# A Mamba-2 state-space branch, computed with channels instead of time steps on the partitions

## The chip, the core and the metric

The kernel runs on one core of a Trainium2 chip. A core has five engines that run at the same time, each working off its own instructions in order: TensorE multiplies matrices (in the profile PE, its weight loads PEld), VectorE (DVE) and ScalarE (ACT) do elementwise work, GpSimd (POOL) does elementwise work on the on-chip memory SBUF only, and SyncE (SP) issues DMAs. ACT can issue DMAs too. A matrix product writes into the accumulators, PSUM, and reads both operands from SBUF. SBUF and PSUM have 128 partitions; a tile `128x512` has 512 elements on each of them. In a product the *stationary* operand is loaded into the array first and the *moving* operand then streams through it. The metric is the time of one execution in microseconds (us).

## What is computed

One residual layer over 256 tokens of 2048 channels. A normalised input `h` is projected by one large matrix; the columns go to three branches (stick-breaking attention, a state-space branch, attention into 256 memory tokens), each branch is projected back to 2048 channels, the three are merged with sigmoid gates, and a last projection, a residual add and a norm follow. The change concerns the state-space branch. It has 32 heads of 64 channels in 8 groups of 4 heads (so a group is 256 channels), and one chunk of all 256 tokens:

```python
xbc = silu(causal_depthwise_conv(ssd_xbc, conv_w, conv_b))       # x, B, C
dt  = softplus(ssd_dt + dt_bias);  a = -exp(a_log)
xs  = x * dt[..., None];           a_cum = cumsum(dt * a)        # over time
decay_in = exp(where(tri, a_cum[l] - a_cum[s], -inf))
cb     = einsum('lgn,sgn->gls', C, B)
y      = einsum('gls,gels,sgep->lgep', cb, decay_in, xs)
y      = y + d_skip * x
g      = y * silu(z)
g      = g * rsqrt(mean over the group's 256 channels of g*g + eps) * ssd_norm_w
branch = g @ w_branch_ssd
```

The weights are f32. A large product is made exact by splitting both operands into a high and a low part (`wh`, `wl`; type f32r) and adding three products.

## The kernel before

**Chunks and pumps.** All weights stream from DRAM. A *chunk* is 512 KB of weights: SP loads it into one of four `raw` buffers (`load_chunk`, L205), ACT writes its high part `wh` (L144), DVE the low part `wl` (L148: `raw` minus `wh`), each into one of three buffers, and PE multiplies. `gemm` (L247) takes chunks of 2 x 128 input channels by 512 outputs and puts tokens on the partitions of the result; the activations are stationary, the weights move: twelve matmuls of 512 columns (L264 to L266). `gemm_cols` (L209) takes 4 x 128 input channels by 256 outputs and puts output channels on the partitions; the weights are stationary: eight matmuls of 512 columns (L227) and eight of 256 (L231). After each chunk's matmuls the program calls `pump` (L183), so a *pump* is the place between two chunks where other work is put into the engines' queues.

**Lanes.** Side work is written as generators. `pump` first runs what was deferred to this pump (`defer`), then advances one of two lanes, odd and even pumps in turn, by one step, up to the next `yield`. Where a generator ends, the next in its lane starts in the same advance. `finish` (L191) runs both lanes to their end at once.

**State space before.** `z` comes from four `gemm` of 8 chunks, evacuated by rows into `zD` (L675); `x`, `B`, `C` come from `gemm_cols`, go through the convolution and SiLU and stand by channels in `cT`. `dt_steps` (L447) leaves `dts` (dt), `nac` (minus the cumulated decay), `edge` (two exponentials of it) by time, and the cumulated decays by heads in DRAM, `acT`. `start_ssd`, eight pumps after the convolution's last chunk, fills each lane with four groups (`ssd_group`, L713), then four `ssd_cols` (L790).

A group takes nine advances: (1) transpose `x` into `xp` and load decays of all 256 tokens, spread over the partitions, through ACT's DMA queue; (2) copy `xp` (ACT), form `xs`, the skip term and `xoff` on POOL, multiply B and C into `cb`; (3) eight additions with minimum on DVE (L751); (4) Exp on ACT; (5) multiply by `cb`, masked, on DVE; (6) the products `y`, decays stationary, 64 columns of `xs` moving (L769), for each head two diagonal blocks of 128 x 128 tokens; what the first half of the tokens gives the second goes through `off` for the four heads together (L771); (7) add up and multiply by `z`, DVE; (8) squares with their sum on ACT, then on POOL mean plus epsilon (L137) and the power -0.5 (L138), `128x2`; (9) scale into `zD` (L786). `ssd_cols` transposes the finished rows back to channels on PE (`dot`, L799) and splits them with the norm's weight into `oD`, the operand of the branch's product. It starts when all eight groups are done.

**Around it.** During this the main program runs the loop over branches (L849): for each of four column blocks a gate `gemm` over `hT` (8 chunks) and a branch `gemm` (4, 4 and 8 chunks for memory, attention and state space). Ahead of the third branch stands `finish()` (L851), since that branch reads `oD`.

Of the kernel before, what the change touches and what calls it, by code (L numbers as in the profile page):

```python
# [10 lines left out]
F32 = mybir.dt.float32  # L11
F32R = mybir.dt.float32r
# [29 lines left out]
def trunk_kernel(  # L42
# [3 lines left out]
    d_skip, w_mem_kv, w_branch_sb, w_branch_ssd, w_branch_mem,  # L46
# [46 lines left out]
    wcols = const.tile([P, 192], F32, name="wcols")  # L93
    normw, ssdw, convb = wcols[:, 0:16], wcols[:, 16:32], wcols[:, 32:64]
    convw = wcols[:, 64:192].rearrange("p (j i) -> p j i", i=32)

# [27 lines left out]
    drow = const.tile([P, SSD_HEADS], F32, name="drow")  # L124

# [6 lines left out]
    edge = const.tile([P, 2, SSD_HEADS], F32, name="edge")  # L132
# [222 lines left out]
    def along(k):  # L355
# [14 lines left out]
        if k == 6:  # L370
            nc.sync.dma_start(wcols, w_cols)
            nc.sync.dma_start(drow, d_skip.partition_broadcast(P))
# [74 lines left out]
    def dt_steps():  # L447
# [54 lines left out]
        nc.vector.tensor_tensor(edge[:, 0], nac[:, 0], ps[:, 2], ALU.subtract)  # L502
        nc.vector.tensor_scalar(edge[:, 1], nac[:, 1], -1.0, None, ALU.mult)
        nc.scalar.activation(edge, edge, AF.Exp)
# [165 lines left out]
    zD = [slot([P, D], F32, "zD") for _ in range(2)]  # L670

    def z_evac(c0):
        def evac(acc):
            for t in range(2):
                nc.scalar.activation(zD[t][:, c0:c0 + GW], acc[t], AF.Copy)  # L675
        return evac

    for g in range(4):
        gemm(hT, NKT, w_in, C_SSDZ + g * GW, z_evac(g * GW))
# [20 lines left out]
    waiting = [zD[i // 2][:, (i % 2) * 1024:(i % 2 + 1) * 1024] for i in range(4)]  # L700
# [12 lines left out]
    def ssd_group(g):  # L713
        heads = slice(4 * g, 4 * g + 4)
        cs = slice(g * T, (g + 1) * T)
        xp = bank([P, 2, T], "xp")
        for b in range(2):
            i = 2 * g + b
            for t in range(2):
                nc.tensor.transpose(xp[:, t, b * P:(b + 1) * P],  # L720
                                    cT[i // 8][:, i % 8, t * P:(t + 1) * P], ident)
        dec = []
        for h0 in (4 * g, 4 * g + 2):
            d = ta([P, 2, 2, P], "dec")
            nc.scalar.dma_start(d.rearrange("p h q t -> p h (q t)"),
                                acT[h0:h0 + 2].partition_broadcast(P))
            dec.append(d)
        yield
        xn = tb([P, 2, T], "xn")
        nc.scalar.activation(xn, xp, AF.Copy)  # L730
        xs = tb([P, 2, T], "xs")
        xe = tq([P, 3, P], "xe")
        by_head = lambda a: a.rearrange("p (h c) -> p h c", c=64)
        wide = lambda a: a[:, heads].unsqueeze(2).to_broadcast([P, 4, 64])
        xoff = xe[:, 0:2].rearrange("p a b -> p (a b)")
        for t in range(2):
            nc.gpsimd.tensor_tensor(by_head(xs[:, t]), by_head(xn[:, t]), wide(dts[:, t]),
                                    ALU.mult)
            nc.gpsimd.tensor_tensor(by_head(xn[:, t]), by_head(xn[:, t]), wide(drow), ALU.mult)
        nc.gpsimd.tensor_tensor(by_head(xoff), by_head(xs[:, 0]), wide(edge[:, 0]), ALU.mult)  # L740
        cb = bank([P, 4, P], "cb")
        bT, cTT = cT[2], cT[3]
        nc.tensor.matmul(cb[:, 0:2], bT[:, g, 0:P], cTT[:, g], start=True, stop=True)
        nc.tensor.matmul(cb[:, 2], bT[:, g, P:T], cTT[:, g, P:T], start=True, stop=True)
        yield

        for i, d in enumerate(dec):
            for e in range(2):
                for q in range(2):
                    h = 4 * g + 2 * i + e  # L750
                    nc.vector.tensor_scalar(d[:, e, q], d[:, e, q], nac[:, q, h:h + 1], 0.0,  # L751
                                            ALU.add, ALU.min)
        yield
        for d in dec:
            nc.scalar.activation(d, d, AF.Exp)
        yield
        nc.scalar.activation(xe[:, 2], cb[:, 1], AF.Copy)
        cbm = small2([P, 2, P], "cbm")
        nc.vector.tensor_tensor(cbm, cb[:, 0:3:2], past.unsqueeze(1).to_broadcast([P, 2, P]),
                                ALU.mult)  # L760
        for d in dec:
            nc.vector.tensor_tensor(d, d, cbm.unsqueeze(1).to_broadcast([P, 2, 2, P]),
                                    ALU.mult)
        yield
        y = bank([P, 2, T], "y")
        for e in range(4):
            xc = slice(e * 64, (e + 1) * 64)
            for q in range(2):
                nc.tensor.matmul(y[:, q, xc], dec[e // 2][:, e % 2, q], xs[:, q, xc], start=True, stop=True)  # L769
        off = bank([P, T], "off")  # L770
        nc.tensor.matmul(off, xe[:, 2], xoff, start=True, stop=True)  # L771
        yield
        nc.vector.tensor_tensor(by_head(xoff), by_head(off), wide(edge[:, 1]), ALU.mult)
        nc.vector.tensor_tensor(xn[:, 1], xn[:, 1], xoff, ALU.add)
        nc.vector.tensor_tensor(xn, y, xn, ALU.add)
        ss = small([P, 2], "gss")
        for t in range(2):
            nc.vector.tensor_tensor(xn[:, t], xn[:, t], zD[t][:, cs], ALU.mult)
        yield
        for t in range(2):  # L780
            nc.scalar.activation(xs[:, t], xn[:, t], AF.Square, accum_out=ss[:, t:t + 1])
        rs = small([P, 2], "grs")
        rsqrt_mean(rs, ss, T, 2)
        yield
        for t in range(2):
            nc.scalar.activation(zD[t][:, cs], xn[:, t], AF.Copy, scale=rs[:, t:t + 1])  # L786
        ssd_done.append(g)
        yield

    def ssd_cols(g):  # L790
# [4 lines left out]
        ot = bank([P, 2, T], "dot")  # L795
        for b in range(2):
            c = (2 * g + b) * P
            for t in range(2):
                nc.tensor.transpose(ot[:, b, t * P:(t + 1) * P], zD[t][:, c:c + P], ident)  # L799
        yield  # L800
        split(*[(*oD[0].at(2 * g + b), ot[:, b], ssdw[:, 2 * g + b:2 * g + b + 1])
                for b in range(2)])
# [141 lines left out]
_INS = ['x', 'mem', 'x_cols', 'mem_cols', 'w_cols', 'w_in', 'b_gate', 'dt_bias', 'a_log', 'd_skip',  # L944
# [5 lines left out]
def lay_out(inputs):  # L950
# [8 lines left out]
    for name in ('x', 'mem'):  # L959
        a[name + '_cols'] = a[name].T.reshape(NKT, P, T).transpose(1, 0, 2).reshape(P, -1)  # L960
    a['mem_cols'] = _np.concatenate([a['mem_norm_w'].reshape(-1, P).T, a['mem_cols']], axis=1)
    a['w_cols'] = _np.concatenate([a[n].reshape(-1, P).T for n in
                                   ('norm_w', 'ssd_norm_w', 'conv_b', 'conv_w')], axis=1)
# [18 lines left out]
```

## Time and profile before

| | |
|---|---|
| median of 3 runs | 1232.03 us (1231.22 to 1232.85) |
| the profiled execution | 1232.29 us |
| its span, first to last instruction | 1230.6 us |
| granted TensorE clock, mean | 0.998 |
| busy: DVE, ACT, POOL | 769.0, 617.2, 92.2 us |
| DMA moved | 240.58 MB, mean 196 GB/s |

The page of the profile gives busy times and the chain of work that ended last; the chain is followed back from the last instruction, at each step to what released it. A group of instructions is written `line engine op out<-in`. In the timeline each row has start, duration, engine, line, operation, tiles, shape and count, and in brackets the idle time before it with what ended it. Matmuls are pipelined: a row's duration is longer than the distance to the next start, and it is the distance that adds up. A product of two f32 operands appears as two records in a trace, a transpose as one. A row of a line's own view has the shortest, median and longest duration in ns, then first and last start.

### The profile page before, as it was taken

What the parts mean: (1) busy time and instruction counts of PE and PEld (TensorE: products, weight loads), DVE (VectorE), ACT (ScalarE), POOL (GpSimd) and SP (SyncE); (2) the same over time, 40 slices, a digit from 0 to 9 for tenths busy, and PEclk for the clock granted to TensorE, in tenths of its full rate; (3) what the DMA queues carried; (4) which work ended last, traced back from release to release, by engine and by line L of the source; (5) the groups of instructions that cost most, each with busy time, mean ns of one, the idle gap of its engine ahead of it and who ended that gap; (6) DMA issues with size and microseconds to landing.
All of it is one profiled execution on the core that took longest, in us unless ns stands there. A gap on an engine that the chain in (4) does not pass through costs nothing.

```text
span 1230.6 us, 16254 instructions
## 1 busy us (share of the span) xinstructions
PE 1220.5 (99%) x6228; PEld 1037.9 (84%) x6228; DVE 769.0 (62%) x999; ACT 617.2 (50%) x797; POOL 92.2 (7%) x104
## 2 busy tenths in 40 slices
PE   9999999999999999999999999999999999999997
PEld 7888888888888888888888888888888888888886
DVE  5686554565654555888878767576756554555554
ACT  6765544554444554545664655455555444444443
POOL 0000000000000000010000202123101110110101
PEclk9999999999999999999999999999999999999999
DMA  9966566655566665655666756666565666567673
GB/s 339 334 198 188 163 195 189 187 168 166 165 183 191 178 177 179 184 176 171 178 182 201 226 178 207 204 191 198 180 186 180 198 197 200 187 197 243 205 243 109
DMA packets 165789, 240.58 MB, mean 196 GB/s; under 512 B 10288, under 2 KB 93392, under 8 KB 165584
## 3 DMA queue, kind: packets, MB, share of 16 engines
q1 hardware_dynamic: 157152, 223.88, 58.9%
q10 hardware_dynamic: 8560, 15.67, 3.8%
q8 instruction: 48, 0.79, 0.3%
q14 instruction: 29, 0.24, 0.1%
HBM read 237.40 MB, written 2.13 MB: 195 GB/s over the span
## 4 chain that ended last, share of the span: by engine, by line
PE 95%; DMA 2%; issue 1%; ACT 1%; DVE 1%; SPq 0%; POOLq 0%; POOL 0%; ACTq 0%
PE acc L227 24%; PE acc L264 17%; PE acc L266 17%; PE acc L265 17%; PE acc L231 12%; PE y L769 1%; PE acc L400 1%; PE acc L401 1%; PE acc L399 1%; DMA raw<-in_w_out_dram 1%; DMA rows<-in_mem_dram 1%; DMA raw<-in_w_mem_kv_dram 0%; PE off L771 0%; PE dtp L459 0%; PE dot L799 0%
## 5 line engine op out<-in xcount | busy, mean ns | idle before, releaser
L148 DVE TENSOR_TENSOR wl<-raw,wh 128x1024 fp32r<-128x1024 f32 (+1 forms) x409 | 506.0, 1240 | 326.4 <-ACT wh L144 324.1
L144 ACT ACTIVATE wh<-raw 128x1024 fp32r<-128x1024 f32 (+1 forms) x409 | 431.5, 1056 | 423.7 <-PE acc L266 253.7
L227 PE MATMUL acc<-hT,wh 128*128 128x512 f32 x1152 | 363.2, 397 | 0.0
L231 PEld LDWEIGHTS acc<-hT,wl 128*128 128x128 f32 x1152 | 216.4, 188 | 51.2
L264 PE MATMUL acc<-wh,hT 128*128 128x512 f32 x576 | 227.8, 395 | 0.0
L231 PE MATMUL acc<-hT,wl 128*128 128x256 f32 x1152 | 226.5, 278 | 0.0
L266 PE MATMUL acc<-wh,hT 128*128 128x512 f32 x576 | 224.5, 390 | 0.0
L265 PE MATMUL acc<-wl,hT 128*128 128x512 f32 x576 | 224.4, 390 | 0.0
L227 PEld LDWEIGHTS acc<-hT,wh 128*128 128x128 f32 x1152 | 175.5, 189 | 0.1
L266 PEld LDWEIGHTS acc<-wh,hT 128*128 128x128 f32 x576 | 108.1, 188 | 22.9
L265 PEld LDWEIGHTS acc<-wl,hT 128*128 128x128 f32 x576 | 108.3, 188 | 21.8
L264 PEld LDWEIGHTS acc<-wh,hT 128*128 128x128 f32 x576 | 108.2, 188 | 21.7
L265 PE MATMUL acc<-wl,oD 128*128 128x512 f32 x128 | 49.8, 389 | 0.0
L266 PE MATMUL acc<-wh,oD 128*128 128x512 f32 x128 | 49.8, 389 | 0.0
L264 PE MATMUL acc<-wh,oD 128*128 128x512 f32 x128 | 49.8, 389 | 0.0
L695 DVE SCALAR_TENSOR_TENSOR cT<-cu,wcols,cT 128x255 f32<-128x255 f32 (+2 forms) x96 | 46.4, 483 | 3.4
L841 POOL TENSOR_TENSOR merged<-merged,sig 128x512 f32<-128x512 f32 x16 | 27.5, 1743 | 260.7 <-DVE sig L840 233.9
L631 POOL TENSOR_TENSOR lm<-lm,sp 128x384 f32<-128x384 f32 x8 | 11.5, 1432 | 394.5 <-DVE sp L630 392.4
L227 PE MATMUL acc<-memT,wh 128*128 128x512 f32 x128 | 40.6, 398 | 0.0
L264 PE MATMUL acc<-wh,mT 128*128 128x512 f32 x96 | 37.4, 390 | 0.0
L266 PE MATMUL acc<-wh,mT 128*128 128x512 f32 x96 | 37.4, 389 | 0.0
L265 PE MATMUL acc<-wl,mT 128*128 128x512 f32 x96 | 37.4, 389 | 0.0
(250 smaller groups left out, 1306.1 us busy)
## 6 DMA issues: line engine op xcount, KB each, us to landing
raw<-in_w_in_dram SPq DMA_DIRECT2D x288, 512.0 KB, 3.8
raw<-in_w_branch_ssd_dram SPq DMA_DIRECT2D x32, 512.0 KB, 4.0
raw<-in_w_out_dram SPq DMA_DIRECT2D x32, 512.0 KB, 4.9
raw<-in_w_mem_kv_dram SPq DMA_DIRECT2D x31, 512.0 KB, 6.3
raw<-in_w_branch_mem_dram SPq DMA_DIRECT2D x16, 512.0 KB, 4.8
raw<-in_w_branch_sb_dram SPq DMA_DIRECT2D x16, 512.0 KB, 4.3
dec<-acT ACTq DMA_DIRECT2D x16, 256.0 KB, 5.6
sig<-in_b_gate_dram ACTq DMA_DIRECT2D x12, 256.0 KB, 3.9
```

Source lines behind the costliest of these rows:

```text
L144: nc.scalar.activation(hi, src, AF.Copy, **({} if scale is None else {"scale": scale}))
L148: nc.vector.tensor_tensor(lo, src, h32, ALU.subtract)
L227: nc.tensor.matmul(halves[b], wh[:, kt - k0, b * P:(b + 1) * P], lhs.both(kt), start=first, stop=False, skip_group_check=True)
L231: nc.tensor.matmul(halves[b][:, 1], wl[:, kt - k0, b * P:(b + 1) * P], lhs.at(kt)[0], start=False, stop=last, skip_group_check=True)
L264: nc.tensor.matmul(a, lh[:, tt], wh[:, j], start=first, stop=False)
L265: nc.tensor.matmul(a, lh[:, tt], wl[:, j], start=False, stop=False)
L266: nc.tensor.matmul(a, ll[:, tt], wh[:, j], start=False, stop=last)
L399: nc.tensor.matmul(a, lh[:, tt], wh[:, g], start=first, stop=False)
L400: nc.tensor.matmul(a, lh[:, tt], wl[:, g], start=False, stop=False)
L401: nc.tensor.matmul(a, ll[:, tt], wh[:, g], start=False, stop=last)
L695: nc.vector.scalar_tensor_tensor(a[:, s:T], u[:, 0:T - s], convw[:, 3 - s, i:i + 1], a[:, s:T], ALU.mult, ALU.add)
L841: nc.gpsimd.tensor_tensor(merged[t][:, cs], merged[t][:, cs], sig[:, t], ALU.add)
```

## The change

`z` is now computed by `gemm_cols` into `zT`, channels on the partitions, with the fold of two accumulators that `to_cols` does (a copy on ACT, an add on DVE). For each head three decay tiles of 128 x 128 are made, the third (first half of the tokens to second) in place of `off`; `edge` goes and `nacx` (`nac` of the first half less its end) comes. In the products `y` the 64 channels of a head in `xs` are stationary and the decays move; the even head of a pair writes partitions 0 to 63 of the result and the odd one 64 to 127. The result stands by channels, so that the skip term is one instruction per 128 channels with a per-partition scalar `dcol` (a column of `wcols`; the load of `drow` goes). The sum of squares over a group's channels is a product with a matrix of ones (`rb`, split operands `sq`), which gives `128x256` with all rows equal; DVE forms mean plus epsilon, POOL the power -0.5 over all 256 columns, DVE multiplies. POOL's five products a group go. `ssd_cols` only splits. A group takes eleven advances and each `ssd_cols` one. The decays are loaded by five DMAs a group from SP's queue instead of two from ACT's. `finish()` moves behind the third branch's first gate `gemm`.

```diff
-    for g in range(4):
-        gemm(hT, NKT, w_in, C_SSDZ + g * GW, z_evac(g * GW))
+    zT = [slot([P, 8, T], F32, "zT") for _ in range(2)]
+    for g in range(8):
+        gemm_cols(hT, NKT, w_in, C_SSDZ + 2 * g * P, to_cols(zT[g // 4], 2 * (g % 4)))
...
     def ssd_group(g):
...
+        dec = [ta([P, 4, P], "dec"), ta([P, 4, P], "dec"), tb([P, 4, P], "dec")]
+        block = lambda e, j: dec[e][:, j] if e < 3 else dec[j][:, 3]
+        for e in range(3):
+            nc.sync.dma_start(dec[e][:, 0:2].rearrange("p q t -> p (q t)"),
+                              acT[heads[e]:heads[e] + 1].partition_broadcast(P))
+        for j in range(2):
+            nc.sync.dma_start(dec[j][:, 3:4], acT[heads[3]:heads[3] + 1,
+                                                  j * P:(j + 1) * P].partition_broadcast(P))
...
+        nc.vector.tensor_tensor(by_head(xs), by_head(xp), dts[:, :, heads[0]:heads[0] + 4]
+                                .unsqueeze(3).to_broadcast([P, 2, 4, 64]), ALU.mult)
+        cbm = small2([P, 3, P], "cbm")
+        nc.scalar.activation(cbm[:, 1], cb[:, 1], AF.Copy)
+        nc.vector.tensor_tensor(cbm[:, 0:3:2], cb[:, 0:3:2],
+                                past.unsqueeze(1).to_broadcast([P, 2, P]), ALU.mult)
+        def log_decays(e):
+            for j, i, a in ((2, 1, nac[:, 1]), (1, 1, nacx), (0, 0, nac[:, 0])):
+                nc.vector.tensor_scalar(block(e, j), block(e, i), a[:, heads[e]:heads[e] + 1],
+                                        0.0, ALU.add, ALU.min)
+        def weigh(i):
+            nc.vector.tensor_tensor(dec[i][:, 0:3], dec[i][:, 0:3], cbm, ALU.mult)
+            nc.vector.tensor_tensor(dec[i][:, 3], dec[i][:, 3], cbm[:, i], ALU.mult)
+        log_decays(0)
+        yield
+        for e in (3, 1, 2):
+            log_decays(e)
+        nc.scalar.activation(dec[0], dec[0], AF.Exp)
+        yield
+        nc.scalar.activation(dec[1], dec[1], AF.Exp)
+        nc.scalar.activation(dec[2], dec[2], AF.Exp)
+        weigh(0)
+        yield
+        weigh(1)
+        weigh(2)
         yield
         y = bank([P, 2, T], "y")
-        for e in range(4):
-            xc = slice(e * 64, (e + 1) * 64)
-            for q in range(2):
-                nc.tensor.matmul(y[:, q, xc], dec[e // 2][:, e % 2, q], xs[:, q, xc], start=True, stop=True)
-        off = bank([P, T], "off")
-        nc.tensor.matmul(off, xe[:, 2], xoff, start=True, stop=True)
+        for b in range(2):
+            pair = [(e, y[64 * (e % 2):64 * (e % 2) + 64, b]) for e in (2 * b, 2 * b + 1)]
+            xe = lambda e, t: xs[:, t, 64 * e:64 * e + 64]
+            for e, o in pair:
+                if e < 3:
+                    nc.tensor.matmul(o, xe(e, 0), dec[e][:, 0:2], start=True, stop=False,
+                                     skip_group_check=True)
+                else:
+                    for j in range(2):
+                        nc.tensor.matmul(o[:, j * P:(j + 1) * P], xe(e, 0), block(e, j),
+                                         start=(j == 0), stop=False, skip_group_check=True)
+            for e, o in pair:
+                nc.tensor.matmul(o[:, P:T], xe(e, 1), block(e, 2), start=False, stop=True,
+                                 skip_group_check=True)
+        yield
+        for b in range(2):
+            i = 2 * g + b
+            nc.vector.scalar_tensor_tensor(xT[b], xT[b], dcol[:, i:i + 1], y[:, b], ALU.mult,
+                                           ALU.add)
+        xg = cT[g // 4][:, 2 * (g % 4):2 * (g % 4) + 2]
+        nc.vector.tensor_tensor(zg, zg, xg, ALU.mult)
+        yield
+        nc.scalar.activation(xs, zg, AF.Square)
+        nc.vector.tensor_tensor(xs[:, 0], xs[:, 0], xs[:, 1], ALU.add)
+        yield
+        sq = tmp.tile([P, 2, T], F32R, tag="tq", name=nm("sq"), bufs=2)
+        split((sq[:, 0], sq[:, 1], xs[:, 0], None))
+        yield
+        tot = bank([P, T], "tot")
+        for i in range(2):
+            nc.tensor.matmul(tot, rb, sq[:, i], start=(i == 0), stop=(i == 1))
+        yield
+        nc.vector.tensor_scalar(xs[:, 0], tot, 1.0 / T, EPS, ALU.mult, ALU.add)
+        nc.gpsimd.tensor_tensor(xs[:, 1], xs[:, 0], mhalf[:, 0:1].to_broadcast([P, T]), ALU.pow)
+        yield
+        nc.vector.tensor_tensor(zg, zg, xs[:, 1:2].to_broadcast([P, 2, T]), ALU.mult)
         ssd_done.append(g)
...
     def ssd_cols(g):
...
-        ot = bank([P, 2, T], "dot")
-        for b in range(2):
-            c = (2 * g + b) * P
-            for t in range(2):
-                nc.tensor.transpose(ot[:, b, t * P:(t + 1) * P], zD[t][:, c:c + P], ident)
-        yield
-        split(*[(*oD[0].at(2 * g + b), ot[:, b], ssdw[:, 2 * g + b:2 * g + b + 1])
-                for b in range(2)])
+        split(*[(*oD[0].at(i), zT[i // 8][:, i % 8], ssdw[:, i:i + 1])
+                for i in (2 * g, 2 * g + 1)])
         yield
...
     for br, (g0, src, nk, wb) in enumerate(branches):
-        if br == 2:
-            finish()
-            mT.append(Cols(NKT, "mT"))
-            src = oD[0]
         for g in range(4):
             sig = t4([P, 2, GW], "sig")
             gemm(hT, NKT, w_in, C_GATE + g0 + g * GW, gate_evac(g0 + g * GW, sig))
+            if src is None:
+                finish()
+                mT.append(Cols(NKT, "mT"))
+                src = oD[0]
             gemm(src, nk, wb, g * GW, branch_evac(br, g, sig))
```

More of the change, by code (lines that the diff above doesn't have):

```diff
@@ L713, in ssd_group @@
     def ssd_group(g):
[L714 to L715 removed]
+        heads = range(4 * g, 4 * g + 4)
+        xT = [cT[i // 8][:, i % 8] for i in (2 * g, 2 * g + 1)]
+        zg = zT[g // 4][:, 2 * (g % 4):2 * (g % 4) + 2]
+        dec = [ta([P, 4, P], "dec"), ta([P, 4, P], "dec"), tb([P, 4, P], "dec")]
[6 more added lines that the diff above has]
+                                                  j * P:(j + 1) * P].partition_broadcast(P))
         xp = bank([P, 2, T], "xp")
         for b in range(2):
[L718 removed]
             for t in range(2):
[L720 to L727, printed above, removed]
[L728 to L741 removed]
+                nc.tensor.transpose(xp[:, t, b * P:(b + 1) * P], xT[b][:, t * P:(t + 1) * P],
+                                    ident)
+        cb = bank([P, 3, P], "cb")
         bT, cTT = cT[2], cT[3]
```

58 lines of the change are left out of this document (12 added, 46 removed).

## The prediction

> **What bounds the kernel now.** I read the page first: engine sums, then the chain that ended last.
>
> ```profile
> span 1230.6 us, 16254 instructions
> ...
> PE 1220.5 (99%) x6228; PEld 1037.9 (84%) x6228; DVE 769.0 (62%) x999; ACT 617.2 (50%) x797; POOL 92.2 (7%) x104
> ...
> PE 95%; DMA 2%; issue 1%; ACT 1%; DVE 1%; SPq 0%; POOLq 0%; POOL 0%; ACTq 0%
> ```
>
> PE is busy throughout and holds 95% of the chain: what adds or takes PE time moves the end, and other engines count only if PE comes to wait for them. Next I read the timeline of PE, ACT and DVE around one group's `y` (columns: start, duration, engine, line).
>
> ```profile
> 712.26 0.39 PE L266 MATMUL acc<-wh,hT 128*128 128x512 f32 x1
> 712.49 0.39 PE L264 MATMUL acc<-wh,hT 128*128 128x512 f32 x1
> ...
> 714.98 0.39 PE L266 MATMUL acc<-wh,hT 128*128 128x512 f32 x1
> 715.21 1.89 PE L769 MATMUL y<-xs,dec 128*128 128x64 f32 x16
> 716.94 0.65 PE L771 MATMUL off<-xe 128*128 128x256 f32 x2
> 717.24 0.59 PE L264 MATMUL acc<-wh,hT 128*128 128x512 f32 x1
> 717.66 0.40 PE L265 MATMUL acc<-wl,hT 128*128 128x512 f32 x1
> ```
>
> ```profile
> 712.69 1.06 ACT L144 ACTIVATE wh<-raw 128x1024 fp32r<-128x1024 f32 x1 [1.66 <-PE acc L266]
> ```
>
> ```profile
> 713.78 1.23 DVE L148 TENSOR_TENSOR wl<-raw,wh 128x1024 fp32r<-128x1024 f32 x1 [1.49 <-ACT wh L144]
> ```
>
> A `gemm` chunk is 12 matmuls at 0.227 us (712.49 to 714.98 is eleven steps): 2.72 us. ACT's split waits for the chunk that frees its buffer (three of `wh`, `wl`); DVE's half ends at 715.01, 2.52 us after the chunk that follows the freed one began at 712.49. PE wants that `wl` two chunks and one matmul after 712.49, 5.67 us: **slack 3.15 us**. Until PE waits, DVE may be held that long.
>
> **The change, part by part: PE.** What goes and its nearest neighbours:
>
> ```profile
> 908.81 0.39 PE L266 MATMUL acc<-wh,hT 128*128 128x512 f32 x1
> 909.04 0.60 PE L799 MATMUL dot<-ident,zD 128*128 128x128 f32 x4
> 909.39 0.48 PE L264 MATMUL acc<-wh,oS 128*128 128x512 f32 x1
> 909.71 0.40 PE L265 MATMUL acc<-wl,oS 128*128 128x512 f32 x1
> ```
>
> ```profile
> 692.09 0.59 PE L743 MATMUL cb<-cT,cT 128*128 128x256 f32 x2
> 692.52 0.38 PE L744 MATMUL cb<-cT,cT 128*128 128x128 f32 x2
> 692.66 0.47 PE L264 MATMUL acc<-wh,oM 128*128 128x512 f32 x1
> 692.97 0.39 PE L265 MATMUL acc<-wl,oM 128*128 128x512 f32 x1
> ```
>
> Removed: `y` and `off` push the chunk after them from 714.98 to 717.66 less two steps, 2.23 us a group, 17.8 us for eight. The `dot` transposes likewise: 909.71 less 908.81 less two steps, 0.45 us, 3.6 us for eight. Together 21.4 us.
>
> Added, `y` by channels: an f32 matmul is two records. Per record, 256 columns take 0.215 us (692.09 to 692.52, two) and 128 take 0.112 us (692.52 to 692.97 less one step, two). A group issues three matmuls of 256 columns (six records) and six of 128 (twelve): in file 6 x 0.215 + 12 x 0.112 = 2.63 us. The two heads of a pair write different partitions of one bank through different halves of the array. If two halves can always run together it is half, 1.32 us. In program order a matmul's second record waits for the first in the same half, and only the second overlaps the neighbour's first; stepping through the eighteen records so gives about 1.66 us. No row shows two halves at once. I take 1.66 us, 13.3 us for eight, with ends 10.5 and 21.0 us.
>
> ```profile
> 108.78 0.39 PE L231 MATMUL acc<-hT,wl 128*128 128x256 f32 x2
> 109.01 1.07 PE L459 MATMUL dtp<-hT,wd 128*64 128x256 f32 x8
> 109.92 0.63 PE L227 MATMUL acc<-hT,wh 128*128 128x512 f32 x2
> ```
>
> A stationary operand of 64 columns is in this trace: `dtp` starts 0.23 us after a pair that takes 0.23 us, and its eight matmuls end on 0.91 us, 0.114 each. Entering and leaving costs nothing visible, and I add nothing. The Trainium skill, "TensorEngine Tiling (Array Packing)", section Key Properties, says that changing the tiling mode drains the engine: sixteen changes at the excess of a matmul's 0.39 us over its 0.227 us step would be an estimated 2.6 us more, which these rows do not show; the same section says that tiles run in parallel, which would favour the end at 10.5 us.
>
> ```profile
> 303.57 0.63 PE L227 MATMUL acc<-hT,wh 128*128 128x512 f32 x2
> ...
> 306.36 0.28 PE L544 MATMUL mlg<-kT,qM 128*128 128x256 f32 x1
> 306.48 0.28 PE L545 MATMUL mlg<-kT,qM 128*128 128x256 f32 x1
> ```
>
> `z` by channels: 32 chunks of `gemm` become 32 of `gemm_cols`, and one of these lasts 306.36 less 303.57, 2.79 us: 32 x 0.07 = 2.2 us more. `tot`: two matmuls of 256 columns a group at 0.12 us, 1.9 us. The `xp` and `cb` matmuls are the same ones, now together: nothing. **PE's sum: 13.3 + 2.2 + 1.9 - 21.4 = -4.0 us** (-6.8 to +3.7).
>
> **Work with no price while covered.** DVE: `xs`, the log decays and weights of three tiles instead of two.
>
> ```profile
> 696.84 1.65 DVE L751 TENSOR_SCALAR dec<-dec,nac 128x128 f32<-128x128 f32 x8
> ```
>
> ```profile
> 704.54 1.29 DVE L762 TENSOR_TENSOR dec<-dec,cbm 128x512 f32<-128x512 f32 x2
> ```
>
> By these, 0.21 us per 128 columns of decay and 0.65 us per product of 512, the heaviest step (nine decays, 1.86 us) with a split of 1.2 us makes 3.1 us in a 2.72 us chunk; the one before it makes 2.8 us. Both lanes take these in four successive chunks: about 1.0 us behind, inside the slack. With two products of 512 of gate evacuation among them, 1.3 us, it still fits; without cover each us of lag past 3.15 us costs a us.
>
> ACT gains one Exp of 512 columns and loses copies; at 50% it hides that. `z`'s fold adds DVE a product of 512, 0.65 us, eight times, hidden likewise. DMAs: five `dec` loads a group move from ACT's queue to SP's, ahead of later weight loads.
>
> ```profile
> raw<-in_w_in_dram SPq DMA_DIRECT2D x288, 512.0 KB, 3.8
> ...
> dec<-acT ACTq DMA_DIRECT2D x16, 256.0 KB, 5.6
> ```
>
> Bytes are the same. Their buffers were last read by `y` ten pumps earlier, so SP does not stop there; a weight load has four buffers, about 10.9 us, for a landing of 3.8, and one group's `dec` equals one chunk, so 2.7 us more is covered. One `d_skip` load leaves SP's start: nothing. If SP did stop, weights would come late by that wait.
>
> Steps: a group used nine advances of its lane and now uses eleven. First steps fall on pumps 8 and 9 after the convolution; branches one and two end at pump 96. Four groups at eleven advances finish on pumps 96 and 97, the splits into `oD` on 97 to 104, and the gate gemm that now stands ahead of `finish()` holds exactly pumps 97 to 104. So `finish()` finds nothing: no price; a slip by one step would cost about a chunk, 2.7 us.
>
> **The wait that is added: POOL's power.** DVE writes mean plus epsilon as 128x256, POOL raises it to -0.5, DVE multiplies. Before, it was 128x2.
>
> ```profile
> L138 POOL TENSOR_TENSOR grs<-ms,mhalf x8: 688/689/761, 722.6 to 895.4; 128x2 f32<-128x2 f32 x8
> ```
>
> ```profile
> L890 POOL TENSOR_TENSOR frs<-msy,mhalf x2: 670/670/671, 1214.5 to 1223.8; 128x1 f32<-128x1 f32 x2
> ```
>
> ```profile
> L737 POOL TENSOR_TENSOR xs<-xn,dts x16: 607/612/1596, 687.0 to 860.7; 128x256 f32<-128x256 f32 x16
> ```
>
> Bounds for D, one such power: below, a product of the same shape, 0.61 us; above, half of a 128x2 power for each element, 256 x 0.345 = 88 us. Nearest are the two power rows: the second column costs 0.019 us, so D = 0.67 + 255 x 0.019 = **5.5 us** (an estimate from these rows). What matters is what DVE can do meanwhile:
>
> ```profile
> 687.66 0.61 POOL L739 TENSOR_TENSOR xn<-xn,drow 128x256 f32<-128x256 f32 x1
> 688.24 1.59 POOL L737 TENSOR_TENSOR xs<-xn,dts 128x256 f32<-128x256 f32 x1
> ```
>
> ```profile
> 687.88 1.48 DVE L148 TENSOR_TENSOR wl<-raw,wh 128x1024 fp32r<-128x1024 f32 x1 [2.42 <-ACT wh L144]
> ```
>
> ```profile
> 722.61 0.69 POOL L138 TENSOR_TENSOR grs<-ms,mhalf 128x2 f32<-128x2 f32 x1
> ```
>
> ```profile
> 723.07 0.42 DVE L774 TENSOR_TENSOR xn<-xn,xe 128x256 f32<-128x256 f32 x1
> ```
>
> DVE's split, two inputs from SBUF, lasts 1.48 instead of 1.23 us beside POOL, and POOL's next product 1.59 instead of 0.61: they exclude each other, the one that has waited longer going first. Against this, L774 was not held by the tiny power, whose reads are over at once. A power of 256 columns reads throughout, and I take it to hold DVE's splits. The Trainium skill, "SBUF — State Buffer", section Who interferes with whom, says the same, an exclusive lock for the whole instruction; L774 departs from "whole", and by a release after the reads alone the sum would be the first rival's.
>
> Price per pair of groups (two lanes, adjacent chunks), time 0 being the end of the chunk before `tot`: DVE splits until 2.5; first power to 2.5 + D; the held split (1.2) to 3.7 + D; second power to 3.7 + 2D; then DVE's product (0.7) and the next split (1.2), 5.6 + 2D. PE wants that split after four chunks (10.9), two `tot` (0.5), the next group's `xp` and `cb` (0.45 like `dot`, and 692.09 to 692.97 less one step, 0.65) and one matmul, 12.7. Stall 2D - 7.1: nothing up to D = 3.55 us, 3.9 us at 5.5. Four pairs: **16 us**. Queued behind the waiting product are the weight splits, and PE waits for those.
>
> **Sum.** The profiled execution took 1232.3 us (span 1230.6; 0.3 us over the median shown, 1232.03). 1232.3 - 4.0 + 16 = **1244 us**.
>
> **Rivals.**
> 1. The power is short or releases DVE after its reads: no stall, 1228 us (1225 to 1230 with the halves together). For it: L774; slack 3.15 us. It decides below D = 3.55 us. This is the other side, faster.
> 2. As 1, but the array's halves run in file: `y` 21.0 us, 1236 us; the change then does not do what its words promise. For it: no row shows overlap; against: nothing but the separate partitions.
> 3. D between 3.7 and 4.4 us: four stalls of 0.3 to 1.7 us meet PE's gain, 1230 to 1235 us.
> 4. D above 7.8 us: four stalls over 8.5 us, beyond 1262 us; the upper bound, 88 us, would give about 1904.
>
> **Chances.** Forecast (D 4.4 to 7.8 us, 1235 to 1262) 0.38; rival 1 0.34; rival 2 0.11; rival 3 0.10; rival 4 0.07. A measurement here can tell 0.2%, 2.5 us. Faster: rival 1, 0.34. Within: rival 3, 0.10. Slower: the rest, 0.56. The range 1225 to 1261 leaves out rival 4 and the forecast's far edge; the forecast's own is 1235 to 1262.
>
> **What would show it.** POOL's power rows: duration near 5.5 us, and `wl` rows of that length beside them; gaps in PE before L265 about 4 us, four times between the first and the last group. PE's `y` from first start to next chunk: 1.7 us, or 2.6 in file, 1.3 together. `z` chunks at 2.79 us. No PE gap at `finish()`. Wrong would make me: powers under 3.55 us, splits of 1.23 us beside a power, or PE waiting at the decay steps or for a weight load.

## The result and the profile after

The changed kernel takes 1522.01 us (median of 4, 1521.35 to 1523.66) against 1232.44 us (4 runs, 1231.22 to 1233.45): ratio 1.2352, 95% interval 1.2331 to 1.2374. The forecast was 1244 us with a range of 1225 to 1261: the side was right, the size was wrong by 278 us. The profiled execution took 1523.66 us, its span 1521.9 us, with a mean granted clock of 0.909.

From the page of the changed kernel: span, busy time, slices, chain, costliest groups (busy time and mean ns, then the idle time before them with what ended most of it).

```profile
span 1521.9 us, 16517 instructions
...
PE 1237.6 (81%) x6340; PEld 1046.0 (69%) x6340; DVE 799.9 (53%) x1094; ACT 614.1 (40%) x766; POOL 381.6 (25%) x56
...
PE   9999999999999999999812961492188129999997
...
POOL 0000000000000000000497069419915970000011
PEclk9999999999999999999955985696589559999999
...
PE 72%; POOL 14%; issue 9%; DVE 2%; ACT 2%; DMA 1%; SPq 0%; POOLq 0%; ACTq 0%; DVEq 0%
...
L793 POOL TENSOR_TENSOR xs<-xs,mhalf 128x256 f32<-128x256 f32 x8 | 328.9, 41121 | 258.0 <-DVE xs L792 258.0
...
L795 DVE TENSOR_TENSOR zT<-zT,xs 128x512 f32<-128x512 f32 x8 | 8.2, 1027 | 300.8 <-POOL xs L793 300.8
```

PE's busy time rose by 17.1 us only, but its idle time (span less busy) went from 10.1 to 284.3 us. The slices show where: four holes in PE, in each of which POOL is busy, and nothing outside them that the slices show. POOL is busy with the power. One takes **41.1 us**, where the prediction took 5.5, and DVE's multiplication L795 waited 300.8 us for eight of them.

From the list of waits of the changed kernel (us in total, times, longest):

```profile
PE acc L264 <- DVE wl L147: 271.7, 11, 36.8
```

In the holes PE doesn't wait for POOL. It waits for `wl`, DVE's half of a weight split: eight long waits, 269.9 us together, and three short ones, 1.8 us. The timelines of POOL, of DVE and of PE at the first pair of groups show how the one becomes the other:

```profile
744.05 82.22 POOL L793 TENSOR_TENSOR xs<-xs,mhalf 128x256 f32<-128x256 f32 x2 [154.53 <-DVE xs L792]
```

```profile
744.35 1.40 DVE L147 TENSOR_TENSOR wl<-raw,wh 128x1024 fp32r<-128x1024 f32 x1 [0.43 <-ACT wh L143]
...
747.34 1.23 DVE L147 TENSOR_TENSOR wl<-raw,wh 128x1024 fp32r<-128x1024 f32 x1 [0.43 <-ACT wh L143]
785.22 1.10 DVE L795 TENSOR_TENSOR zT<-zT,xs 128x512 f32<-128x512 f32 x1 [36.66 <-POOL xs L793]
786.24 1.21 DVE L147 TENSOR_TENSOR wl<-raw,wh 128x1024 fp32r<-128x1024 f32 x1
826.31 0.69 DVE L795 TENSOR_TENSOR zT<-zT,xs 128x512 f32<-128x512 f32 x1 [38.86 <-POOL xs L793]
```

```profile
787.51 0.80 PE L264 MATMUL acc<-wl,hT 128*128 128x512 f32 x1 [31.55 <-DVE wl L147]
788.10 0.63 PE L265 MATMUL acc<-wh,hT 128*128 128x512 f32 x1
788.53 0.63 PE L263 MATMUL acc<-wh,hT 128*128 128x512 f32 x1
```

The split at 747.34 runs inside the first power and lasts its ordinary 1.23 us; the one at 744.35, which begins 0.3 us after the power, lasts 1.40. DVE is not locked out: it has reached its multiplication, whose operand is not there, and everything queued behind it stands still, the weight splits too. Two lanes, two powers one behind the other on POOL, two stalls a pair. After each PE starts again at 0.43 us a matmul in place of 0.227 (788.10 to 788.53); the granted clock is 0.50 from 787.5 to 790.6 us. 79 matmuls behind the eight stalls start late in this way, 17 us together.

The sum of the longer span, 291.3 us, by the distances from start to start beyond a step of 0.227: 271.7 in the eight stalls (this way of counting comes out at the total of all eleven waits by chance), 17 at low clock, 4.4 less of PE's own work (below), together 284. Of the other 7 us, a stall of the kind that the first experiment shows holds 5.5, from 841 to 852 us (4.1 of waiting and 1.4 at low clock behind it); the rest was not itemised.

### The profile page after: what moved, and what is told of

It reads as the page before. It is cut to its first block, busy times and chain, and to the rows that moved or that the text cites. A ratio compares the mean times of both kernels' runs of the same rounds, so it can differ in the third digit from the quotient of the medians.

```text
span 1521.9 us, 16517 instructions
## 1 busy us (share of the span) xinstructions
PE 1237.6 (81%) x6340; PEld 1046.0 (69%) x6340; DVE 799.9 (53%) x1094; ACT 614.1 (40%) x766; POOL 381.6 (25%) x56
## 4 chain that ended last, share of the span: by engine, by line
PE 72%; POOL 14%; issue 9%; DVE 2%; ACT 2%; DMA 1%; SPq 0%; POOLq 0%; ACTq 0%; DVEq 0%
PE acc L226 24%; POOL xs L793 14%; PE acc L230 12%; PE acc L264 10%; PE acc L263 10%; PE acc L265 10%; DVE wl L147 1%; DMA raw<-in_w_mem_kv_dram 1%; PE acc L398 1%; PE acc L399 1%; DMA raw<-in_w_out_dram 1%; PE acc L397 1%; ACT wh L143 1%; PE y L765 0%; PE dtp L457 0%
## 5 line engine op out<-in xcount | busy, mean ns | idle before, releaser
L226 PE MATMUL acc<-hT,wh 128*128 128x512 f32 x1408 | 444.0, 397 | 0.0
L264 PE MATMUL acc<-wl,hT 128*128 128x512 f32 x448 | 183.5, 410 | 270.9 <-DVE wl L147 270.9
L793 POOL TENSOR_TENSOR xs<-xs,mhalf 128x256 f32<-128x256 f32 x8 | 328.9, 41121 | 258.0 <-DVE xs L792 258.0
L230 PEld LDWEIGHTS acc<-hT,wl 128*128 128x128 f32 x1408 | 264.5, 188 | 62.5
L264 PEld LDWEIGHTS acc<-wl,hT 128*128 128x128 f32 x448 | 88.8, 198 | 292.5 <-DVE wl L147 274.4
L230 PE MATMUL acc<-hT,wl 128*128 128x256 f32 x1408 | 276.8, 278 | 0.0
L226 PEld LDWEIGHTS acc<-hT,wh 128*128 128x128 f32 x1408 | 214.5, 189 | 0.1
L263 PE MATMUL acc<-wh,hT 128*128 128x512 f32 x448 | 182.7, 408 | 1.7 <-ACT wh L143 1.7
L265 PE MATMUL acc<-wh,hT 128*128 128x512 f32 x448 | 181.4, 405 | 0.0
L795 DVE TENSOR_TENSOR zT<-zT,xs 128x512 f32<-128x512 f32 x8 | 8.2, 1027 | 300.8 <-POOL xs L793 300.8
L263 PEld LDWEIGHTS acc<-wh,hT 128*128 128x128 f32 x448 | 88.3, 197 | 21.9 <-ACT wh L143 2.1
L265 PEld LDWEIGHTS acc<-wh,hT 128*128 128x128 f32 x448 | 88.7, 198 | 18.9
```

Source lines behind the costliest of these rows:

```text
L226: nc.tensor.matmul(halves[b], wh[:, kt - k0, b * P:(b + 1) * P], lhs.both(kt), start=first, stop=False, skip_group_check=True)
L230: nc.tensor.matmul(halves[b][:, 1], wl[:, kt - k0, b * P:(b + 1) * P], lhs.at(kt)[0], start=False, stop=last, skip_group_check=True)
L263: nc.tensor.matmul(a, lh[:, tt], wh[:, j], start=first, stop=False)
L264: nc.tensor.matmul(a, lh[:, tt], wl[:, j], start=False, stop=False)
L265: nc.tensor.matmul(a, ll[:, tt], wh[:, j], start=False, stop=last)
L793: nc.gpsimd.tensor_tensor(xs[:, 1], xs[:, 0], mhalf[:, 0:1].to_broadcast([P, T]), ALU.pow)
```

## The experiments

Line numbers are each kernel's own. In all of them the kernel before ran on the same chip beside them; its median was 1232.79 us (15 runs) in the first set and 1233.02 us (18 runs) in the second.

**1. The power becomes a product.** The scaling by the root is left out.

```diff
-        nc.gpsimd.tensor_tensor(xs[:, 1], xs[:, 0], mhalf[:, 0:1].to_broadcast([P, T]), ALU.pow)
+        nc.gpsimd.tensor_tensor(xs[:, 1], xs[:, 0], mhalf[:, 0:1].to_broadcast([P, T]), ALU.mult)
```

> The changed kernel with POOL's power replaced by a product of the same 128x256 operands; the scaling by the root mean square is so left out. Theory A (the whole loss is the eight powers of 41.1 us on which DVE's multiplication waits in its queue; PE's sum is -4 to -5 us as the y rows of 1.66 us, the missing dots and the z chunks say): 1226 to 1229 us, no PE gap over 1 us between the first and the last group, granted clock 0.998. Rival B (part of the loss is the heavier DVE work of decays and weights, or the loads on SP's queue): PE still waits at those steps, 1235 us or more.

Measured: 1234.01 us (10 runs, 1230.65 to 1236.57), ratio 1.0005 (0.9994 to 1.0016). One operation of eight instructions held 288 us. But without any power the kernel isn't faster than before either, where the forecast's other terms have it 4 us faster: the time fell between the two expectations. One place in its trace says why; the timelines of PE, ACT and DVE there:

```profile
772.83 0.40 PE L265 MATMUL acc<-wh,oM 128*128 128x512 f32 x1
774.90 0.50 PE L263 MATMUL acc<-wh,hT 128*128 128x512 f32 x1 [1.68 <-ACT wh L143]
776.16 0.50 PE L264 MATMUL acc<-wl,hT 128*128 128x512 f32 x1 [0.76 <-DVE wl L147]
```

```profile
767.50 0.63 ACT L750 ACTIVATE dec<-dec 128x512 f32<-128x512 f32 x1 [3.33 <-DVE dec L739]
...
769.10 1.28 ACT L832 ACT_TABLE_LOAD   x1
770.39 1.06 ACT L832 ACTIVATE sig<-sig 128x1024 f32<-128x1024 f32 x1
...
771.46 1.28 ACT L752 ACT_TABLE_LOAD   x1
...
773.81 1.04 ACT L143 ACTIVATE wh<-raw 128x1024 fp32r<-128x1024 f32 x1
```

```profile
765.34 1.41 DVE L831 TENSOR_TENSOR sig<-acc,sig 128x512 f32<-128x512 f32 x2
```

In the step with the decays of three heads, ACT's Exp of `dec[0]` stands ahead of the chunk's weight split in ACT's queue. DVE forms the other decay in `dec[0]`, that of the fourth head, in the same step, behind the gate's evacuation (765.34), so the Exp waits 3.33 us. Then a sigmoid falls due, with a load of its table and another to return to Exp (1.28 us each), and the next split starts at 773.81, too late for PE: 1.8 and 1.0 us beyond its step. In this execution PE then ran at half clock from 777 to 780 us (granted 0.5). The traces of experiments 2 and 3 have the same two gaps, without low clock behind them.

**2. What a power costs by its columns, and whether it holds DVE.** Ten unused powers early in the run of experiment 1's kernel, where POOL is idle and DVE splits weights.

```diff
+    pw = ta([P, T], "pw")
+    for n in (1, 2, 4, 8, 16, 32, 64, 128, 256):
+        nc.gpsimd.tensor_tensor(pw[:, 0:n], rbc_x[:, 0:n], mhalf[:, 0:1].to_broadcast([P, n]),
+                                ALU.pow)
+    nc.gpsimd.tensor_tensor(pw[:, 0:P], ones[:, 0:P],
+                            mhalf[:, 0:1].to_broadcast([P, P]), ALU.pow)
```

> As e1_mult, and while POOL is idle early on nine powers of 1, 2, 4, 8, 16, 32, 64, 128 and 256 columns of one input and one of 128 columns of ones, whose results nobody reads. Theory A: a power costs about 0.16 us a column over the whole range beyond a few columns, so 128 take 20.6 and 32 take 5.2 us, and the rows of 1 and 2 columns (0.67 and 0.69) lie on a floor; DVE's weight splits beside the long powers last 1.23 us as ever and the time is that of e1_mult. Rival C (my prediction's lock: a power holds DVE's two-input reads for its duration): splits beside the powers last up to the rest of the power, 20 to 40 us, and PE waits there by 50 us or more in sum. Rival D (a step in cost above some size, say a path for large tiles): cost per column below 0.03 us up to that size.

Measured: one execution, 1231.08 us. From the groups of instructions by form, POOL alone:

```profile
L529 POOL TENSOR_TENSOR pw<-rbc_x,mhalf 128x256 f32<-128x256 f32 x1 | 41.1, 41117 | 0.1
L531 POOL TENSOR_TENSOR pw<-ones,mhalf 128x128 f32<-128x128 f32 x1 | 21.5, 21514 | 0.1
L529 POOL TENSOR_TENSOR pw<-rbc_x,mhalf 128x128 f32<-128x128 f32 x1 | 20.8, 20774 | 0.1
L529 POOL TENSOR_TENSOR pw<-rbc_x,mhalf 128x64 f32<-128x64 f32 x1 | 10.5, 10519 | 0.1
L529 POOL TENSOR_TENSOR pw<-rbc_x,mhalf 128x32 f32<-128x32 f32 x1 | 5.5, 5525 | 0.1
...
L529 POOL TENSOR_TENSOR pw<-rbc_x,mhalf 128x1 f32<-128x1 f32 x1 | 1.5, 1467 | 9.9 <-DVE rbc_x L336 9.9
L529 POOL TENSOR_TENSOR pw<-rbc_x,mhalf 128x2 f32<-128x2 f32 x1 | 1.2, 1207 | 0.1
L529 POOL TENSOR_TENSOR pw<-rbc_x,mhalf 128x4 f32<-128x4 f32 x1 | 1.0, 1007 | 0.1
```

From 32 columns up, twice the columns cost twice the time: (41.12 - 20.77) / 128 = **0.16 us a column**. From 1 to 4 columns nothing can be read off the width; the rows even come in falling order (8 and 16 columns, not shown, took 2.6 and 3.2 us). What is raised matters little (ones: 21.51 against 20.77). DVE's splits beside the 256 columns, from the view of the tile `wl` between 110 and 150 us (shortest, median, longest ns):

```profile
L147 DVE TENSOR_TENSOR wl<-raw,wh x12: 1206/1225/1227, 110.9 to 145.7; 128x1024 fp32r<-128x1024 f32 x12
```

Twelve splits, two inputs from SBUF each, and none is longer than 1.23 us while POOL raises 256 columns. The power does not lock DVE out for its length; none of the twelve begins in its first microsecond, where the changed kernel's 744.35 shows a short hold.

**3. The root on ACT.** Mean, epsilon and the power -0.5 become a logarithm, read from PSUM, and an Exp; DVE's and POOL's instructions go (`epsc` is a column that holds epsilon).

```diff
-        nc.vector.tensor_scalar(xs[:, 0], tot, 1.0 / T, EPS, ALU.mult, ALU.add)
-        nc.gpsimd.tensor_tensor(xs[:, 1], xs[:, 0], mhalf[:, 0:1].to_broadcast([P, T]), ALU.pow)
+        nc.scalar.activation(xs[:, 0], tot, AF.Ln, bias=epsc[:, 0:1], scale=1.0 / T)
+        nc.scalar.activation(xs[:, 1], xs[:, 0], AF.Exp, scale=-0.5)
```

> The changed kernel with the power computed on ACT, as Exp of -0.5 times Ln of the mean plus epsilon, read from PSUM, instead of DVE's tensor_scalar and POOL's power. Theory A: two ACT instructions of some 0.45 us in place of 41.1, so 1226 to 1229 us, faster than before by 0.3 to 0.5%. Rival E: Ln brings ACT table loads of 1.28 us with it, at most two a group, 20 us on an engine that is 50% busy, and the split of the weights comes late: 1230 to 1240 us.

Measured: 1237.64 us (5 runs, 1236.8 to 1238.98), ratio 1.0039 (1.0026 to 1.0051). The groups of ACT:

```profile
L794 ACT ACT_TABLE_LOAD x8 | 10.3, 1283 | 0.1
L795 ACT ACT_TABLE_LOAD x8 | 10.3, 1283 | 0.1
```

284 us of the power's cost are gone, but each logarithm and each Exp loads a table: sixteen loads, four at each pair of groups. PE's gaps beyond experiment 1's sum to 4.3 us. The Trainium skill, "ScalarE: Activation LUTs", section Table sets: the hidden batching unit, has the two functions in one set, so that one load would do for both; the rows above are against it as long as nothing names that set.

**4. A power of the forecast's own length.** 32 columns are raised and 224 multiplied: 5.4 us of power where the forecast took 5.5.

```diff
-        nc.gpsimd.tensor_tensor(xs[:, 1], xs[:, 0], mhalf[:, 0:1].to_broadcast([P, T]), ALU.pow)
+        nc.gpsimd.tensor_tensor(xs[:, 1, 0:32], xs[:, 0, 0:32],
+                                mhalf[:, 0:1].to_broadcast([P, 32]), ALU.pow)
+        nc.gpsimd.tensor_tensor(xs[:, 1, 32:T], xs[:, 0, 32:T],
+                                mhalf[:, 0:1].to_broadcast([P, T - 32]), ALU.mult)
```

> The changed kernel with POOL's power on 32 of the 256 columns and a product on the other 224; the scaling of those tokens is so left out. This sets the power near the 5.5 us on which the prediction was built. Theory A (no lock; DVE's multiplication waits only for the data): the step to the multiplication leaves about 6.7 us for two powers and products in a row, so next to no stall, 1226 to 1232 us. Rival C (the prediction's lock): 2D - 7.1 with D of about 6 us gives 4.9 us for each of four pairs, 1246 us, and splits of more than 3 us beside a power.

Measured: 1239.59 us (4 runs, 1239.4 to 1239.66), ratio 1.0053 (1.004 to 1.0067): 5.6 us over experiment 1, where the lock would have cost some 15 (2 x 5.42 - 7.1 = 3.7, four times). DVE's timeline at the first pair of groups:

```profile
746.66 1.22 DVE L147 TENSOR_TENSOR wl<-raw,wh 128x1024 fp32r<-128x1024 f32 x1 [0.43 <-ACT wh L143]
749.35 0.72 DVE L798 TENSOR_TENSOR zT<-zT,xs 128x512 f32<-128x512 f32 x1 [1.47 <-POOL xs L795]
749.99 1.21 DVE L147 TENSOR_TENSOR wl<-raw,wh 128x1024 fp32r<-128x1024 f32 x1
755.25 0.69 DVE L798 TENSOR_TENSOR zT<-zT,xs 128x512 f32<-128x512 f32 x1 [4.05 <-POOL xs L795]
```

Both splits run beside a power without loss, and DVE's waits of 1.5 and 4.1 us cost PE nothing here: in the first two pairs of groups it has no gap. In the last two it has five, of 4.3 us together beyond their steps, and experiment 1's stall is 1.3 us longer: 5.6 us, the whole difference. So this test fell between its two expectations: no lock, but a power of this length isn't free either. Why the later pairs alone pay was not tried; gate products stand between the splits in DVE's queue there, and POOL's gate products hold a split for 2.30 us (895.21), though in experiment 1 one lasts as long (890.71) with no gap behind it.

**5. The two repairs together.** Experiment 3 with the table set named once a pair of groups, and the fourth head's decays a step earlier.

```diff
         log_decays(0)
+        log_decays(3)
         yield
-        for e in (3, 1, 2):
+        for e in (1, 2):
             log_decays(e)
...
+        if g % 2 == 0:
+            nc.scalar.preload_act_table_set("natural_log_exp_and_others")
         nc.scalar.activation(xs[:, 0], tot, AF.Ln, bias=epsc[:, 0:1], scale=1.0 / T)
```

> As e3_lnexp, with the two edits that its and e1's profiles point to: one table set that holds Ln and Exp is loaded ahead of Ln (20 loads in the program where e3 has more than 30), and the fourth head's log decays are made one step earlier, so that the Exp of the first tile waits for nothing made in its own step. Theory F (what e1 and e3 lost beside the power is ACT coming late to a weight split: it waited 3.3 us for DVE's decays and then for two table loads, and PE 3.0 us for ACT): no PE gap over 1 us between the first and the last group, 1226 to 1229 us, faster than before by 0.3 to 0.5%. Rival G (the decay work of three tiles is too much for DVE wherever it stands): the gap comes back one step earlier, 1230 to 1234 us.

Measured: **1228.54 us** (5 runs, 1226.87 to 1230.33), ratio 0.9964 (0.9952 to 0.9977): 0.4% under the kernel before, clear of the interval, and under the changed one by far. ACT's timeline at the place of experiment 1's stall:

```profile
765.01 1.28 ACT L837 ACT_TABLE_LOAD   x1
...
767.38 1.28 ACT L755 ACT_TABLE_LOAD   x1
768.67 0.63 ACT L755 ACTIVATE dec<-dec 128x512 f32<-128x512 f32 x1
...
769.73 1.04 ACT L145 ACTIVATE wh<-raw 128x1024 fp32r<-128x1024 f32 x1
```

The same two loads and the same two Exps stand there, but no wait ahead of them, and PE has no gap above 0.5 us from 680 to 1200 us. Of the sixteen loads at the roots four are left, one for each pair of groups.

**6. The order alone.** Experiment 1's kernel with only the fourth head's decays a step earlier, the first five lines of the diff above.

> As e1_mult (POOL multiplies instead of raising to a power, scaling left out), with the fourth head's log decays one step earlier and nothing else. Theory F: the two PE gaps of 2.1 and 1.3 us near 773 us go, and with them the spell of lower clock behind them: 1226 to 1228 us. Rival G: they stay or move, 1230 us or more.

Measured: 1228.44 us (6 runs, 1227.48 to 1231.98), ratio 0.9966 (0.9955 to 0.9977): 5.6 us under experiment 1. The two ran on different chips; by the ratios to the kernel before beside each, the difference is 0.4%, some 5 us. In the trace PE has neither gap nor low clock from 600 to 1200 us. One step of one instruction group is the whole difference between "no gain" and the forecast's gain without a stall (1228 us, the prediction's first rival).

**7. `y` head by head.** In experiment 5 the products of a pair alternate: even head, odd head. Here all of the even head's come first.

```diff
                         nc.tensor.matmul(o[:, j * P:(j + 1) * P], xe(e, 0), block(e, j),
                                          start=(j == 0), stop=False, skip_group_check=True)
-            for e, o in pair:
                 nc.tensor.matmul(o[:, P:T], xe(e, 1), block(e, 2), start=False, stop=True,
                                  skip_group_check=True)
```

> As e5_fix, with the products y issued head by head (all of the even head, then all of the odd head of a pair) instead of in turn. Theory H (each half of the array works off its own matmuls, whatever stands between them in the program): y rows from first start to the next chunk stay at 1.46 us and the time is that of e5_fix. Rival I (matmuls start in program order and only neighbours in different halves run together): about 1.0 us more a group, 2.4 us, and 7 to 8 us more in sum, 1234 us or more.

Measured: 1229.43 us (5 runs, 1228.11 to 1229.83), ratio 0.997 (0.9958 to 0.9982). PE's timeline of one group:

```profile
716.44 0.39 PE L267 MATMUL acc<-wh,hT 128*128 128x512 f32 x1
716.76 0.66 PE L768 MATMUL y<-dec,xs 128*64 128x256 f32 x4
...
718.27 0.50 PE L265 MATMUL acc<-wh,hT 128*128 128x512 f32 x1
718.60 0.40 PE L266 MATMUL acc<-wl,hT 128*128 128x512 f32 x1
```

From 716.44 to 718.60 less two steps of 0.227 is 1.71 us, against 1.66 in the alternating order. In file it would have been near 2.6. So a half of the array starts its next product while the other half is still at work on earlier ones, though they stand in one queue.

**8. `finish()` where it was.** Experiment 5 with `finish()` again ahead of the third branch's first gate `gemm`.

```diff
+        if br == 2:
+            finish()
+            mT.append(Cols(NKT, "mT"))
+            src = oD[0]
         for g in range(4):
             sig = t4([P, 2, GW], "sig")
             gemm(hT, NKT, w_in, C_GATE + g0 + g * GW, gate_evac(g0 + g * GW, sig))
-            if src is None:
-                finish()
-                mT.append(Cols(NKT, "mT"))
-                src = oD[0]
             gemm(src, nk, wb, g * GW, branch_evac(br, g, sig))
```

> As e5_fix, with finish() back ahead of the third branch's first gate gemm. Theory J (the move of finish() carries the two more steps of a group: without it the splits of all sixteen column blocks, about 0.49 us each on ACT and 0.48 on DVE, stand ahead of the next weight split): PE waits 4 to 7 us at that place, 1231 to 1236 us. Rival K (buffers hide it): the time of e5_fix.

Measured: 1235.09 us (10 runs, 1233.53 to 1237.81), ratio 1.0017 (1.0007 to 1.0026): 6.5 us over experiment 5. ACT's timeline and PE's at that place:

```profile
948.56 2.09 ACT L145 ACTIVATE oD<-zT,wcols 128x256 fp32r<-128x256 f32 x5
...
950.56 4.49 ACT L145 ACTIVATE oD<-zT,wcols 128x256 fp32r<-128x256 f32 x11
954.95 2.94 ACT L145 ACTIVATE wh<-raw 128x1024 fp32r<-128x1024 f32 x3
```

```profile
952.16 0.39 PE L267 MATMUL acc<-wh,oS 128*128 128x512 f32 x1
956.04 0.50 PE L265 MATMUL acc<-wh,hT 128*128 128x512 f32 x1 [3.50 <-ACT wh L145]
957.30 0.79 PE L266 MATMUL acc<-wl,hT 128*128 128x512 f32 x1 [0.76 <-DVE wl L149]
```

Sixteen splits into `oD` go into ACT's queue at once, the weights' next split behind them. PE loses 3.7 and 1.0 us in this execution, and close to 3 us more at half clock. All sixteen were still to come at that place, as the prediction's count of pumps has it.

## Why the prediction was wrong, and where it was right

**The step that failed is the size of D, the power of 256 columns**: "the second column costs 0.019 us, so D = 0.67 + 255 x 0.019 = 5.5 us". It measures 41.1 us. The slope came from two rows, 128x1 and 128x2, and both lie on the floor where the width doesn't show (experiment 2); the difference of 0.019 us was no price of a column. The other end, 88 us from half of a `128x2` for each element, was nearer by its kind: in the ladder from 32 columns up the price is 0.16 us, and 256 x 0.16 = 41. The prediction had the case, as its fourth rival with 1904 us at the upper end, but with a chance of 0.07 and outside the range. Between bounds of 0.61 and 88 us, a value of 5.5 from one small difference should not have kept nine tenths of the chance below 8 us.

**The mechanism was named half right.** That PE would wait for `wl`, because DVE's queue stands at the waiting product with the weight splits behind it, is what happened. That the power also holds DVE's splits for its whole length, which the formula 2D - 7.1 for a pair counts, did not happen: the split inside it takes 1.23 us, here and in experiment 2. It holds DVE at its start alone. The splits that begin some 0.3 us after the four first powers take 1.35 to 1.43 us, and beside experiment 1's product of 0.61 us the split at the same place takes 1.40. The prediction's first rival, a release after the reads, fits this, and row L774 had spoken for it; so does experiment 2, where a split that begins 0.3 us into the power of 64 columns isn't held at all (at 78.3 us, 1.23 us long). That the reads end so early is not shown by itself. The Trainium skill, "SBUF — State Buffer", section Who interferes with whom, lets a DVE instruction with two SBUF inputs contend with a POOL instruction that reads SBUF, calls the shared ports an exclusive lock, and describes it, for DVE's two-port modes, as held for the whole instruction. POOL's products of the kernel before agree that the two contend (1.48 in place of 1.23 us); a hold for the whole instruction is not what the 41 us powers show. Without the lock, each split runs beside the power and DVE stops only at the products, which come later than the held split would; the same counting, with the first power starting at 1.1 on the prediction's time scale, gives stalls of D - 9.7 and D - 3.8, together 2D - 13.5 us a pair: 68.7 us at 41.1. This counting was made after the result. PE's long waits of a pair sum to 67.5 us in the mean of the four pairs (269.9 / 4), where the lock would make 75.1. At the forecast's D of 5.5 us this formula gives no stall at all; experiment 4 bears that out for its first two pairs and not for the later ones.

**PE's sum was right.** Predicted -4.0 us. Measured parts: `y` 1.66 us a group against 2.23 before, so -4.6; `dot` gone, -3.6; `tot` +1.9; `z` by channels +1.9 over its 32 chunks where 2.2 was predicted. Sum -4.4 us, and experiments 5 and 6 come out 4.5 us under the kernel before. The timeline of PE in the changed kernel:

```profile
717.69 0.39 PE L265 MATMUL acc<-wh,hT 128*128 128x512 f32 x1
718.01 0.65 PE L765 MATMUL y<-dec,xs 128*64 128x256 f32 x4
...
719.46 0.50 PE L263 MATMUL acc<-wh,hT 128*128 128x512 f32 x1
719.80 0.39 PE L264 MATMUL acc<-wl,hT 128*128 128x512 f32 x1
```

The 1.66 us that were taken for `y` are what is measured (717.69 to 719.80 less two steps), but its make-up isn't, and that the total agrees is luck. The halves overlap almost wholly: 718.01 to 719.46 is 1.45 us, near the 1.32 of the lower end, and some 0.2 us are lost at entering (718.01 is 0.09 us beyond its step) and leaving (0.34 us to 719.80, 0.11 beyond). The prediction had put no price on these, from `dtp`. Most of the loss at leaving follows `cb` as well, where no tiling changes (692.66 to 692.97 in the prediction's rows, 0.08 beyond a step). The Trainium skill, "TensorEngine Tiling (Array Packing)", section Key Properties, says that tiles run in parallel and that a change of tiling mode drains the engine. The trace agrees with the first, with 1.45 us where 2.63 would be in file; for the second it leaves some 0.1 us a group, about 1 us in all, where the prediction's estimate beside that page was 2.6.

**What had been costed at nothing.** ACT "hides that" was wrong at one place: the Exp waits for DVE within one step, and with two table loads behind it the weight split is late (2.9 us beyond PE's steps, and 5.6 us between experiments 1 and 6 with the clock that follows). The prediction named "PE waiting at the decay steps" among the signs that would make it wrong, but put no price on it. A smaller wait of the same Exp, 2.0 us, makes the changed kernel's only other gap at the decays, 0.45 us at 703 us; with the order mended both are gone, so DVE's decays fit into its slack, as predicted. The DMAs on SP's queue cost PE nothing: its list of waits names none of them. `finish()` found nothing to wait for, as predicted, and experiment 8 shows the price of the other place: 6.5 us.

**The clock was not in the sum.** No stall in the kernel before was long enough to show what follows one. Each of the eight here cost 2.1 us more after its end (17 / 8).

## What to carry to other kernels

Before an operation is widened, its price by the element is taken from a wide row, not from the difference of two narrow ones; with no wide row, the whole span between the ends belongs into the range. A wait in an in-order queue is priced by what stands behind it: here eight results that nobody needed soon held up the weights of the whole kernel. And when work is dealt out into steps, an instruction that waits for another engine's work of the same step should come a step later, above all ahead of something that the bound engine needs.

## What the runs showed of the hardware that was not expected

- POOL's power costs 0.16 us a column of 128 (41.1 us for 256), its product of the same shape 0.61: a factor of 67.
- A power of 41 us holds up DVE's splits, which read two operands out of SBUF, only at its start: 1.35 to 1.43 us in place of 1.23, and 1.21 to 1.23 further on. POOL's products of 0.61 us hold them as long (1.40), its gate products longer (2.30).
- The two column halves of the array go through one queue nearly independently: head by head 1.71 us, alternating 1.66.
- After 32 to 37 us of idle time PE works for 3.6 to 5.7 us with 0.427 us a matmul in place of 0.227; after gaps of 2 to 4 us it did so in some executions (experiments 1, 4 and 8) and not in others (2 and 3).
- A logarithm followed by an Exp took two table loads of 1.28 us unless the set that has both was named; then one did for two groups (experiments 3 and 5).
